# Where the low halves are made, and a fixed run of projections in front of the inverse's merging matmuls

## The chip, the core and the metric

The kernel runs on one NeuronCore of a Trainium2 chip. TensorE (PE in the profile) multiplies matrices, VectorE (DVE), ScalarE (ACT) and GpSimd (POOL) work element by element, and SyncE (SP) issues the DMA transfers. Time is device microseconds (us) of the whole program, the median of several runs.

## The reference, cut to what matters

The program is a hybrid block of two layers over 768 tokens (512 latent, 256 context) with 1024 channels. All four mixers read slices of one input projection:

```python
for layer in range(DEPTH):                 # DEPTH = 2
    need_ctx = layer < DEPTH - 1
    u_c, gate_c = modulate(h_ctx, cond_ctx, norm_w[layer], ada_w[layer], ada_b[layer])
    u_l, gate_l = modulate(h_lat, cond_lat, norm_w[layer], ada_w[layer], ada_b[layer])
    pc = split_in(u_c @ in_w[layer])
    pl = split_in(u_l @ in_w[layer])
    ya_c, ya_l = rwkv_branch(...)          # RWKV-7 on r, k, v
    ...                                    # SSD, Hyena, retention
    h_lat = h_lat + gate_l * merge_branches(u_l, ys_l, *mix_args)
```

The RWKV branch runs a recurrence over the tokens, and adds a bonus to what it reads out:

```python
def step(s, inp):
    r_t, w_t, kk_t, b_t, k_t, v_t = inp
    sa = -jnp.einsum('bhvk,bhk->bhv', s, kk_t)
    s = s * w_t[:, :, None, :] + sa[..., None] * b_t[:, :, None, :] + v_t[..., None] * k_t[:, :, None, :]
    return s, jnp.einsum('bhvk,bhk->bhv', s, r_t)
...
coef = jnp.sum(rwkv_heads(r)[:, :, None] * k_h * r_k, axis=(2, 4))
bonus = coef[..., None] * rwkv_heads(v)
```

## The kernel before, in words

**Projections.** `dense` multiplies the activations (kept as a high and a low half, `uh` and `ul`) by one 1024x128 block of weights at a time. `weights` loads half a block (256 KB, `wraw`), ScalarE casts it to the high half (`whi`, L185), and the engine `self.wl` subtracts it from the raw weights, which is the low half (`wlo`, L186). `self.wl` is GpSimd (`self.G`) while the projections are streamed, and VectorE in the merge at each layer's end. Three products (`whi` by `uh`, `whi` by `ul`, `wlo` by `uh`) are summed in PSUM: the 512 latent tokens in the tile `dl`, the 256 context tokens in `dc`. A projection of both segments is 24 matmuls of 128x512 and 24 of 128x256. `stream` then takes the result out of PSUM, with ScalarE alone (L436) or ScalarE and VectorE (L413, L425), and stores it.

**RWKV.** `rwkv_ct` handles one of four channel tiles (ct 0 to 3) per layer, in three stretches.
1. *Preparation:* VectorE and TensorE make the decayed keys and the blocks of A.
2. *Window:* VectorE turns A around (four transposes, L618), inverts all triangular 32x32 blocks by 60 dependent elimination operations (L622 and L623 in turn) and turns the result (L627 for `TT`, L632 for `TB`). The merging matmuls `cc<-TB,A` on TensorE can only start when `TB` is there.
3. *Chunk loop:* 12 chunks in series; each goes TensorE, ScalarE (`Rs`, L672), TensorE, ScalarE (L678), TensorE, VectorE (the state `Z`, L687 and L688), TensorE.

The bonus needs a head sum: a matmul with a matrix of ones (L370), one per segment, whose result VectorE multiplies by `v` (L609). The head sums lie in the PSUM tag `d1`, which has one buffer, so each one can be written only after the one before it was read. Layer 0 has two segments here, layer 1 only the first.

**What sets the order.** A scheduler of the framework orders the instructions of each engine; the order of the code is their priority, and `high_priority(offset=500)` pulls the splits ahead. Each engine then works through its list strictly in order. In the code, `rwkv` streams the next tile's k, r, v and the gate `ga` after each channel tile, and the 41 other projections of layer 0 after all four. Those carry the remaining modulation weights along (`each`): 64 loads of 256 KB (`adr`, four buffers), each cast by ScalarE (`adh`), subtracted by VectorE (`adl`) and used by two matmuls (L302, L303); two of them go with each projection.

Of the kernel before, what the change touches and what calls it, by code (L numbers as in the profile page):

```python
# [7 lines left out]
F32 = mybir.dt.float32  # L8
# [6 lines left out]
NOSYNC = mybir.DependencyInfo(mybir.DependencyClass.NoSync, mybir.DependencyReason.DATA)  # L15
# [124 lines left out]
class K:  # L140
# [56 lines left out]
            self.split(hi[:], lo[:], raw[:], leng=self.wl)  # L197
        return hi, lo

    def dense(self, srcs, uh, ul, segs, M=128):  # L200
        out = {t0: self.pst("dl" if n > 256 else "dc", [128, n]) for t0, n in segs}
        nk = len(srcs) * 4
        for j, src in enumerate(srcs):
            hi, lo = self.weights(src, 4, M)
            for t0, n in segs:
                for kk in range(4):
                    k = j * 4 + kk
                    for p, (w, u) in enumerate(((hi, uh), (hi, ul), (lo, uh))):
                        self.P.matmul(out[t0][:M, :n], w[:, kk, :], u[:, k, t0:t0 + n], start=(k == 0 and p == 0), stop=(k == nk - 1 and p == 2))  # L209
        return out  # L210

    def proj(self, l, ti, segs):
# [176 lines left out]
    def stream(self, l, need_ctx, items, each=None):  # L389

        V, S, G = self.V, self.S, self.G
        both = [(0, 512), (512, 256)]
        osegs = both if need_ctx else both[:1]

        def fg():
            return self.tile(self.fpool, [128, T], F32, "fg")

        for nm, j in items:
            sg = osegs if nm in ("r", "hy", "C", "rq", "ga", "gh", "zs", "gr", "mg") else both
            n1 = sg[-1][0] + sg[-1][1]  # L400
            if nm == "mg":
# [6 lines left out]
            ps = self.dense([src[:, 0:4], src[:, 4:8]], self.uh, self.ul, sg, M)  # L408
            g = fg()
            if nm in ("ga", "gh", "zs", "gr"):  # L410
                for t0, n in sg:
                    S.activation(out=g[:, t0:t0 + n], in_=ps[t0][:], func=AF.Tanh, scale=0.5)
                    V.scalar_tensor_tensor(out=g[:, t0:t0 + n], in0=g[:, t0:t0 + n], scalar=1.0, in1=ps[t0][:], op0=ALU.add, op1=ALU.mult)  # L413
            elif nm == "mg":
                self.gate(g, ps, sg, j)
            elif nm in ("r", "k", "v"):
                xp = self.padded(ps, sg)
                jj = "rkv".index(nm) * 4 + j
                t = fg()
                G.tensor_tensor(out=t[:, 0:512], in0=xp[:, 0:512], in1=xp[:, 2:514], op=ALU.add)  # L420
                if len(sg) > 1:
                    G.tensor_tensor(out=t[:, 512:768], in0=xp[:, 514:770], in1=xp[:, 516:772], op=ALU.add)
                for t0, n in sg:
                    S.activation(out=g[:, t0:t0 + n], in_=ps[t0][:], func=AF.Copy, scale=self.dc[:, jj:jj + 1])
                V.scalar_tensor_tensor(out=g[:, :n1], in0=t[:, :n1], scalar=self.dc[:, 12 + jj:13 + jj], in1=g[:, :n1], op0=ALU.mult, op1=ALU.add)  # L425
            elif nm == "hy":
                self.conv3(self.padded(ps, sg), sg, g, self.col("hcw", 3 * j), self.col("hcw", 3 * j + 1), self.col("hcw", 3 * j + 2), self.col("hcb", j))
            elif nm in ("x", "B", "C"):
                jj = dict(x=0, B=4, C=6)[nm] + j
                self.conv3(self.padded(ps, sg), sg, g, self.col("scw", 3 * jj), self.col("scw", 3 * jj + 1), self.col("scw", 3 * jj + 2), self.col("scb", jj))  # L430
                t = fg()
                S.activation(out=t[:, :n1], in_=g[:, :n1], func=AF.Tanh, scale=0.5)
# [5 lines left out]
            if each:  # L438
                each()
# [6 lines left out]
    def rwkv(self, l, need_ctx, pa, pb, items):  # L446
        segs = [(0, 512), (512, 256)]
        osegs = segs if need_ctx else segs[:1]
        self.load_rwkv(pb)
        for ct in range(4):  # L450
            y, no = self.rwkv_ct(l, ct, need_ctx, pa, pb, segs, osegs)
            self.stream(l, need_ctx, items[ct])
            self.apply_gate(self.fetch(l, "ga", ct, no, pb, "late"), y, no)
            self.nc.sync.dma_start(out=self.yd[0, ct, :, :no], in_=y[:, :no])

# [37 lines left out]

    def rwkv_ct(self, l, ct, need_ctx, pa, p, segs, osegs):
        V, S, G = self.V, self.S, self.G
        no = T if need_ctx else 512
        r = self.fetch(l, "r", ct, no, pa, "r")
        k = self.fetch(l, "k", ct, T, pa, "k")
# [768 lines left out]
    def run(self):  # L1267
        tc = self.tc

        def pool(name, side="left", **kw):  # L1270
            return tc.tile_pool(name=name, bufs=1, reuse_waits="tile", side=side, **kw)

        with tc.tile_pool(name="const", bufs=1) as self.cpool, tc.tile_pool(name="layer", bufs=1) as self.lpool, tc.tile_pool(name="w", bufs=1) as self.wpool, \
# [5 lines left out]
            self.pd = {n: [self.tile(dp, [c, 128, T] if n != "dt" else [16, T], F32, f"pd{n}{l}") for l in range(2)]  # L1279
                       for n, c in (("r", 4), ("k", 4), ("v", 4), ("ga", 4), ("hy", 12), ("x", 4), ("B", 2), ("C", 2), ("rq", 4), ("rk", 4), ("rv", 4),  # L1280
                                    ("gh", 4), ("zs", 4), ("gr", 4), ("dt", 1), ("mg", 32), ("lw", 8), ("la", 8))}
            self.load_consts()
            self.cols2 = [self.tile(self.lpool, [128, NCOLS], F32, f"cols{l}") for l in range(2)]
            self.modc = [self.tile(self.lpool, [128, 24, 2], F32, f"modc{l}") for l in range(2)]
# [4 lines left out]
            items = [[(n, c + 1) for n in "krv"] + [("ga", c)] for c in range(3)] + [[("ga", 3)]]  # L1289

            def some(**kw):
                return [(n, j) for n, c in kw.items() for j in range(c)]

            rest = some(rv=4, rk=4, rq=4, gr=4, gh=4, zs=4) + [("hy", 4 * j + c) for c in range(4) for j in range(3)] + some(dt=1, x=4, B=2, C=2)
# [10 lines left out]
            self.layer_cols(0)  # L1305
            for l in range(2):
                need = l == 0
                self.wl = self.G
                with pool(f"fill{l}") as self.fpool:
                    self.pb = self.PSUM_A  # L1310
                    with pool(f"psA{l}", space=PSUM) as self.psum:
# [24 lines left out]
                        with pool(f"ra{l}") as pa:  # L1336
                            with pool(f"rw{l}") as p:
                                self.rwkv(l, need, pa, p, items)
                        nmg = 0 if need else 2
                        if need:  # L1340
                            with pool("ada") as self.apool:
                                q, todo = [], list(adas)
# [5 lines left out]
                                        if q and (len(q) > 2 or not todo):  # L1348
                                            self.ada_step(*q.pop(0))

                                self.stream(l, need, rest[:4])
                                self.stream(l, need, rest[4:], each)
                                while q:
                                    each()
                        else:
                            self.stream(l, need, rest + [("mg", 24 + j) for j in range(nmg)])
# [54 lines left out]
```

## Time and profile before

| | |
|---|---|
| median of 3 runs | 3113.57 us (3111.22 to 3113.75) |
| the profiled execution | 3116.2 us, its span 3114.4 us |
| mean granted TensorE clock | 0.955 of full speed |
| TensorE busy | 2884.8 us (93%) |
| VectorE busy | 1861.3 us (60%) |
| ScalarE busy | 1174.5 us (38%) |
| GpSimd busy | 784.7 us (25%) |

The span is from the first to the last instruction on the core; 1.8 us of the device time lie around it. An engine counts as busy when it runs anything, at whichever clock. The granted clock (PEclk) is given as a share of full speed; the two levels are 1.2 and 2.4 GHz.

### The profile page before, as it was taken

How to read it: one execution, taken by the hardware profiler on the slowest of the kernel's cores; microseconds unless marked ns; L12 is line 12 of the kernel's file. 1: busy time of each engine (PE TensorE's matmuls, PEld its weight loads, DVE VectorE, ACT ScalarE, POOL GpSimd, SP SyncE). 2: the span in 40 equal slices, each digit the busy share in tenths (PEclk: the TensorE clock that was granted, in tenths of full speed). 3: DMA queues.
4: the chain of work that ended last, by engine and by line, in shares of the span. 5: the costliest groups of instructions: out<-in, count | busy, mean ns of one | idle time of the engine just before them, and what ended most of it. 6: DMA issues, size and time to landing. Idle time of an engine off the chain costs nothing. (4 is left out here: it accounts for less than half of the span.)

```text
span 3114.4 us, 48430 instructions
## 1 busy us (share of the span) xinstructions
PE 2884.8 (93%) x18708; PEld 2328.5 (75%) x18708; DVE 1861.3 (60%) x3288; ACT 1174.5 (38%) x2103; POOL 784.7 (25%) x906
## 2 busy tenths in 40 slices
PE   7998989898999999999999898798989899999898
PEld 3786767677767888777888867677767678877677
DVE  3358382846354577886725445837474535697875
ACT  4643332332354423334422454323333344243432
POOL 3523323232212200111012343332333332011111
PEclk9998989899999999999999988898989899999999
DMA  5542121211374333313425243312131234432434
GB/s 189 193 143 90 52 87 48 92 39 60 105 257 132 118 118 110 102 58 117 134 68 175 94 165 136 102 52 93 60 97 55 78 125 131 137 96 93 144 116 147
DMA packets 164266, 343.24 MB, mean 110 GB/s; under 512 B 19105, under 2 KB 28130, under 8 KB 164036
## 3 DMA queue, kind: packets, MB, share of 16 engines
q1 hardware_dynamic: 164036, 340.15, 33.2%
q8 instruction: 147, 2.41, 0.3%
q14 instruction: 83, 0.68, 0.1%
HBM read 254.77 MB, written 83.74 MB: 109 GB/s over the span
## 5 line engine op out<-in xcount | busy, mean ns | idle before, releaser
L209 PE MATMUL dl<-uh,whi 128*128 128x512 f32 (+1 forms) x1520 | 621.9, 409 | 11.3 <-DVE fg L413 7.1
L209 PE MATMUL dl<-ul,whi 128*128 128x512 f32 (+1 forms) x1520 | 623.9, 411 | 3.7 <-DVE ul L363 3.6
L209 PE MATMUL dl<-uh,wlo 128*128 128x512 f32 (+1 forms) x1520 | 620.3, 408 | 2.4 <-POOL wlo L186 2.4
L186 POOL TENSOR_TENSOR wlo<-wraw,whi 128x512 fp32r<-128x512 f32 (+1 forms) x256 | 348.6, 1363 | 787.7 <-ACT whi L185 693.4
L185 ACT CAST whi<-wraw 128x512 fp32r<-128x512 f32 x452 | 277.8, 615 | 613.4 <-PE dc L209 255.9
L209 PEld LDWEIGHTS dl<-uh,whi 128*128 128x128 f32 (+1 forms) x1520 | 290.8, 191 | 73.1 <-DVE fg L413 8.4
L209 PEld LDWEIGHTS dl<-ul,whi 128*128 128x128 f32 (+1 forms) x1520 | 290.7, 191 | 67.2 <-DVE ul L363 9.3
L209 PEld LDWEIGHTS dl<-uh,wlo 128*128 128x128 f32 (+1 forms) x1520 | 290.5, 191 | 65.9 <-POOL wlo L186 4.1
L209 PE MATMUL dc<-uh,whi 128*128 128x256 f32 (+1 forms) x960 | 282.7, 295 | 22.4 <-DVE fg L413 11.0
L209 PE MATMUL dc<-ul,whi 128*128 128x256 f32 (+1 forms) x960 | 279.4, 291 | 3.8 <-DVE ul L363 3.8
L209 PE MATMUL dc<-uh,wlo 128*128 128x256 f32 (+1 forms) x960 | 279.5, 291 | 0.0
L209 PEld LDWEIGHTS dc<-uh,whi 128*128 128x128 f32 (+1 forms) x960 | 185.3, 193 | 43.7 <-DVE fg L413 12.7
L1211 POOL TENSOR_TENSOR acc<-acc,fg 128x512 f32<-128x512 f32 x72 | 93.2, 1306 | 469.8 <-DVE fg L1210 469.3
L186 DVE TENSOR_TENSOR wlo<-wraw,whi 128x512 fp32r<-128x512 f32 x196 | 145.5, 743 | 107.9 <-ACT whi L185 106.2
L209 PEld LDWEIGHTS dc<-ul,whi 128*128 128x128 f32 (+1 forms) x960 | 185.2, 193 | 18.8 <-DVE ul L363 7.0
L687 DVE TENSOR_TENSOR Z<-cc,Z 128x256 f32<-128x256 f32 x80 | 33.9, 424 | 267.4 <-PE cc L174 267.1
L209 PEld LDWEIGHTS dc<-uh,wlo 128*128 128x128 f32 (+1 forms) x960 | 185.2, 193 | 5.1 <-issue 1.6
L817 POOL TENSOR_TENSOR m<-smask,adl 128x512 fp32r<-128x512 f32 x24 | 33.6, 1401 | 399.7 <-DVE adl L186 269.7
L672 ACT COPY Rs<-cc 64x256 f32<-64x256 f32 x96 | 35.3, 367 | 222.7 <-PE cc L174 221.7
L622 DVE TENSOR_TENSOR KB<-KB 128x30 f32<-128x30 f32 (+14 forms) x240 | 110.0, 458 | 6.4
L623 DVE TENSOR_TENSOR KB<-KB 128x30 f32<-128x30 f32 (+14 forms) x240 | 106.7, 445 | 6.6
L209 PE MATMUL dl<-yh,whi 128*128 128x512 f32 x256 | 103.5, 406 | 4.7 <-ACT yh L185 3.5
(412 smaller groups left out, 5927.9 us busy)
## 6 DMA issues: line engine op xcount, KB each, us to landing
wraw<-in_w SPq DMA_DIRECT2D x248, 256.0 KB, 2.7
wraw<-merge_w SPq DMA_DIRECT2D x128, 256.0 KB, 2.7
adr<-ada_w SPq DMA_DIRECT2D x96, 256.0 KB, 4.1
wraw<-branch_w SPq DMA_DIRECT2D x64, 256.0 KB, 2.7
wraw<-out_w SPq DMA_DIRECT2D x32, 256.0 KB, 3.9
pdlw<-fg SPq DMA_DIRECT2D x16, 384.0 KB, 2.3
pdla<-fg SPq DMA_DIRECT2D x16, 384.0 KB, 3.8
hfd<-Hs SPq DMA_DIRECT2D x16, 384.0 KB, 3.1
```

The costliest lines, as they stand in the source:

```text
L185: (heng or self.S).copy(out=hi, in_=src) if heng is None else heng.tensor_copy(out=hi, in_=src)
L186: (leng or self.V).tensor_tensor(out=lo, in0=src, in1=hi.bitcast(F32), op=ALU.subtract)
L209: self.P.matmul(out[t0][:M, :n], w[:, kk, :], u[:, k, t0:t0 + n], start=(k == 0 and p == 0), stop=(k == nk - 1 and p == 2))
L622: V.tensor_tensor(out=t3, in0=B[:, j + 1:32, j:j + 1].to_broadcast([128, ni, j]), in1=B[:, j:j + 1, 0:j].to_broadcast([128, ni, j]), op=AL ...
L623: V.tensor_tensor(out=B[:, j + 1:32, 0:j], in0=B[:, j + 1:32, 0:j], in1=t3, op=ALU.add)
L672: S.copy(out=Rs[hb], in_=Rp.t[hb])
L687: V.tensor_tensor(out=Zn[:], in0=Zp.t[:], in1=Z[:], op=ALU.add)
L817: eng.tensor_tensor(out=m2[:], in0=self.smask[:, d, :].unsqueeze(1).to_broadcast([128, 4, 128]), in1=ad[:, c, hs:hs + 4].bitcast(F32).unsq ...
L1211: G.tensor_tensor(out=acc[:, oc, t0:t0 + n], in0=acc[:, oc, t0:t0 + n], in1=g[:, t0:t0 + n], op=ALU.add)
```

## The change

It has four parts. The low halves of the streamed projections are made by VectorE. The projections come from one list (a generator, `feed`): k, r, v and `ga`, then six "light" ones per channel tile, then the rest. `fill(us)` issues projections worth that many us (by the formula in `dense_steps`) at a place of the code: one run of them before the bonus's head sum (80 or 54 in layer 0, 60 or 40 in layer 1), a second of 30 behind the transposes that end the inverse. From the head sum to the merging matmuls TensorE follows the order of the code (`manual_schedule`). `dc` becomes one bank used in alternating halves. And the modulation loads go only with those projections that are left when RWKV is done.

```diff
+    def dense_steps(self, out, srcs, uh, ul, segs, M=128):
+        for t0, n in segs:
+            if n > 256:
+                out[t0] = self.pst("dl", [128, n])
+            else:
+                self.ndc += 1
+                out[t0] = self.dcb[:, self.ndc % 2, :n]
...
+                        if n <= 256:
+                            if self.dcl is not None:
+                                self.tc.add_manual_dep(i.ins, self.dcl, NOSYNC, reason="bank order")
+                            self.dcl = i.ins.name
+                yield 12 * n / 2260
...
+    def fill(self, us):
+        while us > 0:
+            c = next(self.feed, None)
+            if c is None:
+                return
+            us -= c
+
+    def require(self, nm, j):
+        while (nm, j) not in self.parked:
+            next(self.feed)
...
             y, no = self.rwkv_ct(l, ct, need_ctx, pa, pb, segs, osegs)
-            self.stream(l, need_ctx, items[ct])
+            self.require("ga", ct)
...
+        self.fill((54 if ct else 80) if need_ctx else (40 if ct else 60))
+        region = self.tc.manual_schedule(engines={mybir.EngineType.PE})
+        region.__enter__()
         cb = self.headsum(ksum, osegs)
...
         V.transpose(out=TB[:].rearrange("p u s -> p s u"), in_=B.rearrange("p t s -> p s t"))
+        self.fill(30)
...
+        region.__exit__(None, None, None)
...
+            self.dcb = self.tile(self.psd, [128, 2, 256], F32, "dc")
...
-                self.wl = self.G
+                self.wl = self.V
...
+                        self.feed = self.stream_steps(l, need, items + [("mg", 24 + j) for j in range(nmg)])
+                        with pool(f"ra{l}") as pa, pool(f"rw{l}") as p:
+                            self.rwkv(l, need, pa, p)
...
-                                self.stream(l, need, rest[:4])
-                                self.stream(l, need, rest[4:], each)
+                                self.each = each
+                                for _ in self.feed:
+                                    pass
                                 while q:
                                     each()
```

TensorE, layer 0, ct 1: the head sum of the bonus (`d<-kd,bones`) for both segments. Before, the first segment stands in the chunk loop of the tile ahead, among its matmuls with `Z`:

```order
L209 MATMUL dl_4767<-uh_141,whi_950_4801 128x512
L209 MATMUL dl_4767<-ul_142,whi_950_4801 128x512
L370 MATMUL d_618_2858<-kd_576_2680,bones_113 128x512
L174 MATMUL cc_2020<-Z_2005,AR_1587 64x128
L174 MATMUL cc_2020<-Z_2005,AR_1680 64x128
```

The second segment stands 255 rows later, between the matmuls that make A, in the preparation.

```order
L174 MATMUL cc_2793<-AR_2777,KB_2778 128x128
L174 MATMUL cc_2804<-AR_2777,KB_2778 128x128 x2
L370 MATMUL d_619_2860<-kd_576_2680,bones_113 128x256
L174 MATMUL cc_2805<-AR_2777,KB_2778 128x128 x2
L174 MATMUL cc_2812<-AR_2777,KB_2778 128x128 x2
```

Now both stand in the window, one behind the other, with 63 projection matmuls of 128x512 and 72 of 128x256 ahead of them in the window and 96 and 84 behind them up to the merging matmuls.

```order
L215 MATMUL dc_111<-uh_142,whi_743_3916 128x256
L215 MATMUL dc_111<-ul_143,whi_743_3916 128x256
L215 MATMUL dc_111<-uh_142,wlo_744_3917 128x256
L386 MATMUL d_745_3946<-kd_650_3327,bones_114 128x512
L386 MATMUL d_746_3948<-kd_650_3327,bones_114 128x256
L215 MATMUL dl_3913<-uh_142,whi_752_4029 128x512
```

VectorE, the same tile: the bonus, which reads those head sums. Before, both readings stand ahead of the transposes that begin the window.

```order
L579 TENSOR_TENSOR A_2667<-cc_2805,maska_1543 128x256
L609 SCALAR_TENSOR_TENSOR bonus_2862<-d_619_2860,v_2649 128x256
L579 TENSOR_TENSOR A_2667<-cc_2812,maska_1543 128x512
L579 TENSOR_TENSOR A_2667<-cc_2813,maska_1543 128x512
L509 TENSOR_SCALAR et_3754<-d_761_3750 128x512
L618 STREAM_TRANSPOSE KB_2865<-A_2667 32x1024 x4
```

Now the first reading stands behind 51 of the 60 elimination operations (L661 and L662 are the old L622 and L623), and six low halves stand among them, the last one shown.

```order
L661 TENSOR_TENSOR KB_3953<-KB_3953 128x130
L186 TENSOR_TENSOR wlo_762_4101<-wraw_760_4098,whi_761_4100 128x512
L648 SCALAR_TENSOR_TENSOR bonus_3950<-d_745_3946,v_3296 128x512
L662 TENSOR_TENSOR KB_3953<-KB_3953 128x5x26
L661 TENSOR_TENSOR KB_3953<-KB_3953 128x108
L662 TENSOR_TENSOR KB_3953<-KB_3953 128x4x27
L648 SCALAR_TENSOR_TENSOR bonus_3950<-d_746_3948,v_3296 128x256
```

TensorE, layer 0, after RWKV: the modulation steps (`adh`, `adl` by `cs`). Before, four of their matmuls follow the 48 of each projection.

```order
L209 MATMUL dc_8326<-uh_141,wlo_1590_8360 128x256
L302 MATMUL d_1564_8226<-adh_8311,cs_54_133 4x512
L303 MATMUL d_1564_8226<-adl_8312,cs_54_133 4x512
L302 MATMUL d_1564_8226<-adh_8319,cs_54_133 4x512
L303 MATMUL d_1564_8226<-adl_8320,cs_54_133 4x512
L209 MATMUL dl_8413<-uh_141,whi_1601_8417 128x512
```

Now the last of them stand alone, pair behind pair, with little else between; the pattern goes on for some 36 of the 64 steps.

```order
L215 MATMUL dc_111<-uh_142,wlo_2422_11864 128x256
L319 MATMUL d_1591_9128<-adl_9142,cs_55_134 4x512
L318 MATMUL d_1591_9128<-adh_9149,cs_55_134 4x512
L319 MATMUL d_1591_9128<-adl_9150,cs_55_134 4x512
L318 MATMUL d_1591_9128<-adh_9157,cs_55_134 4x512
L319 MATMUL d_1591_9128<-adl_9158,cs_55_134 4x512
```

## Rows read from the trace of the kernel before

**Rows 1.** TensorE's waits: line, what it waited for, us in total, times, longest.

```profile
PE cc L174 <- DVE TB L632: 76.1, 8, 14.0
...
PE dc L209 <- DVE fg L413: 11.0, 4, 4.4
...
PE dc L209 <- ACT fg L436: 6.8, 4, 2.9
...
PE d L303 <- DVE adl L186: 3.8, 8, 0.8
```

**Rows 2.** Layer 0's windows: busy us (instructions) by engine; ct 0, ct 3, sum.

```profile
core 0: us, PE busy (x) PEld busy (x) DVE busy (x) ACT busy (x) POOL busy (x), PEclk, DMA share, GB/s
255.30:312.20 56.90, 42.25 (x212) 35.99 (x211) 52.67 (x87) 19.16 (x31) 19.93 (x19) 0.89 0.30 96
...
708.90:749.00 40.10, 29.42 (x169) 24.63 (x168) 38.14 (x74) 9.40 (x16) 9.19 (x9) 0.98 0.20 69
sum 194.00, PE 139.72 PEld 118.88 DVE 184.10 ACT 56.70 POOL 54.19; mean PE 34.93 PEld 29.72 DVE 46.02 ACT 14.18 POOL 13.55
```

**Rows 3.** Layer 0's chunk loops, the same view: ct 0, ct 3, sum.

```profile
312.20:388.80 76.60, 76.56 (x749) 61.09 (x750) 24.55 (x37) 22.91 (x52) 27.27 (x54) 0.92 0.15 51
...
749.00:822.20 73.20, 73.20 (x732) 57.57 (x733) 12.26 (x27) 19.68 (x47) 22.31 (x48) 0.92 0.12 41
sum 300.70, PE 300.61 PEld 237.83 DVE 79.36 ACT 85.21 POOL 102.38; mean PE 75.15 PEld 59.46 DVE 19.84 ACT 21.30 POOL 25.59
```

**Rows 4.** Layer 1's windows, the same view: ct 0 and sum.

```profile
1958.30:2014.50 56.20, 39.66 (x191) 32.06 (x190) 54.58 (x85) 20.76 (x36) 23.68 (x22) 0.87 0.30 97
...
sum 203.70, PE 147.67 PEld 118.94 DVE 196.54 ACT 66.29 POOL 71.76; mean PE 36.92 PEld 29.74 DVE 49.13 ACT 16.57 POOL 17.94
```

**Rows 5.** Layer 1's chunk loop of ct 0, the same view.

```profile
2014.50:2089.10 74.60, 74.53 (x696) 57.38 (x696) 20.22 (x34) 21.35 (x48) 27.95 (x53) 0.92 0.18 57
```

**Rows 6.** Timeline of the end of layer 0's window of ct 1: start, duration, instruction.

```profile
446.24 0.41 DVE L622 TENSOR_TENSOR KB<-KB 128x238 f32<-128x238 f32 x1
...
446.49 1.30 POOL L186 TENSOR_TENSOR wlo<-wraw,whi 128x512 fp32r<-128x512 f32 x1 [2.76 <-ACT whi L185]
...
446.68 1.38 DVE L623 TENSOR_TENSOR KB<-KB 128x238 f32<-128x238 f32 x1
...
447.03 0.39 PE L209 MATMUL dl<-uh,whi 128*128 128x512 f32 x1
...
447.26 0.40 PE L209 MATMUL dl<-ul,whi 128*128 128x512 f32 x1
...
448.09 0.40 DVE L622 TENSOR_TENSOR KB<-KB 128x234 f32<-128x234 f32 x1
...
454.82 0.29 DVE L623 TENSOR_TENSOR KB<-KB 128x130 f32<-128x130 f32 x1
...
457.28 1.90 DVE L627 STREAM_TRANSPOSE TT<-KB 128x1024 f32<-128x1024 f32 x1
...
461.14 2.77 PE L174 MATMUL cc<-TB,A 32*32 32x32 f32 x96 [13.49 <-DVE TB L632]
```

**Rows 7.** GpSimd's low halves (L186) in layer 0's four windows: sum.

```profile
sum 194.00, DVE 0.00 POOL 43.70; mean DVE 0.00 POOL 10.93
```

**Rows 8.** Groups by form: busy us, mean ns | idle before, releaser.

```profile
L186 DVE TENSOR_TENSOR wlo<-wraw,whi 128x512 fp32r<-128x512 f32 x196 | 145.5, 743 | 107.9 <-ACT whi L185 106.2 <-PE dc L209 0.2 <-PE dl L209 0.2
...
L618 DVE STREAM_TRANSPOSE KB<-A 32x1024 f32<-32x1024 f32 x32 | 64.5, 2015 | 3.7 <-PE cc L174 3.4
...
L687 DVE TENSOR_TENSOR Z<-cc,Z 128x256 f32<-128x256 f32 x80 | 33.9, 424 | 267.4 <-PE cc L174 267.1
```

**Rows 9.** The modulation loads: minimum, median, maximum ns; landing in us.

```profile
L185 ACT CAST adh<-adr x64: 605/619/626, 842.1 to 992.8; 128x512 fp32r<-128x512 f32 x64
L186 DVE TENSOR_TENSOR adl<-adr,adh x64: 669/685/1442, 842.7 to 994.5; 128x512 fp32r<-128x512 f32 x64
...
DMA to landing us min/median/max: 2.9/4.1/6.8
```

More of the change, by code (lines that the diff above doesn't have):

```diff
@@ L198, in weights @@
         return hi, lo
-    def dense(self, srcs, uh, ul, segs, M=128):
-        out = {t0: self.pst("dl" if n > 256 else "dc", [128, n]) for t0, n in segs}
+    def dense_steps(self, out, srcs, uh, ul, segs, M=128):
[5 more added lines that the diff above has]
+                out[t0] = self.dcb[:, self.ndc % 2, :n]
         nk = len(srcs) * 4
@@ L208, in dense @@
                     for p, (w, u) in enumerate(((hi, uh), (hi, ul), (lo, uh))):
-                        self.P.matmul(out[t0][:M, :n], w[:, kk, :], u[:, k, t0:t0 + n], start=(k == 0 and p == 0), stop=(k == nk - 1 and p == 2))
+                        i = self.P.matmul(out[t0][:M, :n], w[:, kk, :], u[:, k, t0:t0 + n], start=(k == 0 and p == 0), stop=(k == nk - 1 and p == 2))
+                        if n <= 256:
[3 more added lines that the diff above has]
+                yield 12 * n / 2260
+    def dense(self, srcs, uh, ul, segs, M=128):
+        out = {}
+        for _ in self.dense_steps(out, srcs, uh, ul, segs, M):
+            pass
         return out
@@ L387, in apply_gate, with stream, stream_steps @@
         self.V.scalar_tensor_tensor(out=y[:, :no], in0=g[:, :no], scalar=0.5, in1=y[:, :no], op0=ALU.mult, op1=ALU.mult)
-    def stream(self, l, need_ctx, items, each=None):
+    def fill(self, us):
[7 more added lines that the diff above has]
+            next(self.feed)
+    def stream(self, l, need_ctx, items):
+        for _ in self.stream_steps(l, need_ctx, items):
+            pass
+    def stream_steps(self, l, need_ctx, items):
         V, S, G = self.V, self.S, self.G
@@ L407, in stream @@
             M = 16 if nm == "dt" else 128
-            ps = self.dense([src[:, 0:4], src[:, 4:8]], self.uh, self.ul, sg, M)
+            ps = {}
+            yield from self.dense_steps(ps, [src[:, 0:4], src[:, 4:8]], self.uh, self.ul, sg, M)
             g = fg()
@@ L437, in stream @@
             self.nc.sync.dma_start(out=self.pd[nm][l][j, :, :n1] if nm != "dt" else self.pd[nm][l], in_=g[:M, :n1])
-            if each:
-                each()
+            self.parked.add((nm, j))
+            if self.each:
+                self.each()
     def fetch(self, l, nm, j, n, pool, tag):
@@ L444, in fetch, with rwkv @@
         return t
-    def rwkv(self, l, need_ctx, pa, pb, items):
+    def rwkv(self, l, need_ctx, pa, pb):
         segs = [(0, 512), (512, 256)]
@@ L495, in rwkv_ct @@
         V, S, G = self.V, self.S, self.G
+        for nm in "krv":
+            self.require(nm, ct)
         no = T if need_ctx else 512
@@ L1281, in run @@
                                     ("gh", 4), ("zs", 4), ("gr", 4), ("dt", 1), ("mg", 32), ("lw", 8), ("la", 8))}
+            self.dcb = self.tile(self.psd, [128, 2, 256], F32, "dc")
+            self.ndc, self.dcl = 0, None
             self.load_consts()
@@ L1288, in run @@
             self.cond()
-            items = [[(n, c + 1) for n in "krv"] + [("ga", c)] for c in range(3)] + [[("ga", 3)]]
             def some(**kw):
                 return [(n, j) for n, c in kw.items() for j in range(c)]
-            rest = some(rv=4, rk=4, rq=4, gr=4, gh=4, zs=4) + [("hy", 4 * j + c) for c in range(4) for j in range(3)] + some(dt=1, x=4, B=2, C=2)
+            light = some(rv=4, rk=4, rq=4, gr=4, gh=4, zs=4)
+            items = []
+            for c in range(4):
+                items += [(n, c + 1) for n in "krv" if c < 3] + [("ga", c)] + light[6 * c:6 * c + 6]
+            items += [("hy", 4 * j + c) for c in range(4) for j in range(3)] + some(dt=1, x=4, B=2, C=2)
             adas = [(l, j, k) for l, j0 in ((0, 4), (1, 0)) for j in range(j0, 6) for k in range(8)]
@@ L1307, in run @@
                 need = l == 0
-                self.wl = self.G
+                self.wl = self.V
+                self.parked, self.each = {(n, 0) for n in "krv"}, None
                 with pool(f"fill{l}") as self.fpool:
@@ L1335, in run @@
                                 list(self.hy_filters(1, need, p))
-                        with pool(f"ra{l}") as pa:
-                            with pool(f"rw{l}") as p:
-                                self.rwkv(l, need, pa, p, items)
                         nmg = 0 if need else 2
+                        self.feed = self.stream_steps(l, need, items + [("mg", 24 + j) for j in range(nmg)])
+                        with pool(f"ra{l}") as pa, pool(f"rw{l}") as p:
+                            self.rwkv(l, need, pa, p)
                         if need:
@@ L1349, in each @@
                                             self.ada_step(*q.pop(0))
-                                self.stream(l, need, rest[:4])
-                                self.stream(l, need, rest[4:], each)
+                                self.each = each
+                                for _ in self.feed:
+                                    pass
                                 while q:
                                     each()
+                                self.each = None
                         else:
-                            self.stream(l, need, rest + [("mg", 24 + j) for j in range(nmg)])
+                            for _ in self.feed:
+                                pass
                 acp = pool(f"acc{l}")
```

## Prediction

> **What bounds the kernel now.** I read the shares of the engines first: TensorE is busy for 93% of the span, so the time is TensorE's work plus two losses, its idle time and what the lower clock costs. Next I read its waits, to see which are large. By far the largest is that of the merging matmuls for `TB`: 76.1 us in 8 waits, one per channel tile, up to 14.0 [rows 1]. So I cut the span into windows (from the last preparing matmul to the merging matmuls) and chunk loops. In layer 0's four windows TensorE runs 139.7 of 194.0 us, so 54.3 are idle, while VectorE runs 184.1 [rows 2]; in layer 1 it is 147.7 of 203.7, 56.0 idle, VectorE 196.5 [rows 4]. There VectorE's chain sets the end. In the chunk loops TensorE is busy for 300.6 of 300.7 us [rows 3].
>
> The timeline of one window shows the cause: the last projection matmul starts at 447.26, VectorE goes on alone with the inverse, and merging begins at 461.14 [rows 6]. The projections given to this tile are used up too soon.
>
> The clock is the second loss. A stretch loses its length times what its PEclk lacks; PEclk mixes time at 2.4 GHz with time at 1.2 GHz. In layer 0 the window and the loop of ct 0 lose 56.9x0.11 + 76.6x0.08 = 12.4 us, those of ct 3 40.1x0.02 + 73.2x0.08 = 6.7 [rows 2, 3]; ct 0 of layer 1 loses 56.2x0.13 + 74.6x0.08 = 13.3 [rows 4, 5]. I take their mean, 10.8, for every tile, 43 in each layer, and 6.7 as the price of one cheap fall.
>
> **The windows of layer 0.** The matmuls of a projection start 0.23 us apart for 512 columns (447.03, 447.26 [rows 6]); half of that, 0.114, is my estimate for 256. By the order, TensorE has 178 and 168, 159 and 156, 159 and 156, 156 and 147 of them per window: 53 to 60 us each, while VectorE's work up to `TB` comes to 38 to 48 (below). So `TB` is ready before the merging matmuls, and that wait goes.
>
> But another takes its place. `d1` has one buffer, so the second segment's head sum waits until VectorE has read the first, and it stands in the fixed run, where nothing behind it can pass. VectorE's reading comes late. For ct 1, VectorE must do before it: four transposes, 4x2.015 = 8.1 [rows 8]; 51 of the 60 eliminations; six low halves, 6x0.743 = 4.5 [rows 8]; then the reading itself, 0.7. The eliminations: the last 26 take 457.28-448.09 = 9.2 us, the first 26 have the same sizes, and the 8 in the middle at 0.44 (446.24 to 446.68) make 3.5, in all 21.9; the nine left out take 457.28-454.82 = 2.5 [rows 6], so 19.4. Together 32.7, and VectorE begins 1.3 ahead of the window: 31.4. TensorE comes to the second head sum after 63x0.23 + 72x0.114 + 0.7 = 23.4. It stalls 8.0. In the same way ct 0 (all 60 eliminations, and 3.9 for `TT` and `TB`, ahead of the reading) gives 37.9-27.8 = 10.1; ct 2 (43 eliminations, five gate operations) 31.9-23.4 = 8.5; ct 3 (35, ten other operations) 30.2-21.7 = 8.5. That is 35. I add 5 for GpSimd's remaining interference and small waits: 40 idle against 54.3, a gain of 14.
>
> The clock falls in such stalls as it fell in the old gaps. Four falls at the price of ct 3 (dense work follows each) are 27 against 43, a gain of 16; the bounds are 0 (no better) and 43.
>
> **The windows of layer 1.** There is one segment, so no second head sum. TensorE's projections up to merging are 137 and 120 matmuls, 154 and 48, 154 and 0, 143 and 36: 45.2, 40.9, 35.4 and 37.0 us. VectorE is through `TB` after 8.1 + 21.9 + 3.9, the low halves (6, 9, 11, 11 at 0.743), 0.7 of bonus, and 0, 2, 5, 10 other operations at 0.5 to 1, less 1.3: 37.8, 41.9, 44.0, 46.5. The gaps are 0, 1.0, 8.6 and 9.5, with small waits 22 idle, against 56.0: a gain of 34. Two falls of the clock stay and two mostly go: 12 of the 43 gained, bounds 0 and 22.
>
> **The low halves on VectorE.** Each is cheaper there: GpSimd's last one took 1.30 us, VectorE's mean is 0.743 [rows 6, 8]. But they cost VectorE's time in a window that VectorE bounds; that is in the sums above. What they free is contention: the elimination operation at 446.68 took 1.38 us while GpSimd made a low half (446.49 to 447.79), and one of the same size took 0.41 just before [rows 6]. GpSimd's low halves were 43.7 of its 54.2 us in layer 0's windows [rows 2, 7].
>
> The Trainium skill (SBUF — State Buffer, "Who interferes with whom") states that a VectorE operation with two inputs in SBUF and a GpSimd operation that reads SBUF exclude one another, the later one waiting in full. The 1.38 beside 0.41 agrees. By that rule only the remaining 10.5 us of GpSimd could disturb the eliminations, the 5 I added would be about 2, and the result 3 us lower.
>
> Outside the windows VectorE now has them between the `Z` of the chunk loops: by the order 16, 15 and 14 between one window and the next in layer 0, 16, 18 and 16 in layer 1. VectorE waits 267.4/80 = 3.3 us ahead of each `Z` [rows 8], so most slip in. One that stands just ahead of `Z` delays the serial loop by up to 0.74, and the next tile's preparation, which leaves the windows, stands there too. I take 17 for both layers' loops and preparations; the bounds are 0 and 70 (these 95 at 0.743 in full).
>
> **The halves of `dc`.** In the built program each `dc` matmul still waits for the reading of the other half, so I put this at nothing. If the halves did work alone, the waits of `dc` for readings, 11.0 + 6.8 [rows 1], would go: 18 us more.
>
> **The modulation steps.** Before, each pair of them lay under a projection, and TensorE waited 3.8 us for their low halves [rows 1]. Now some 36 come with hardly a projection (7.5 us in all). Loads have four buffers, and a buffer is free when its subtraction is done: (4.1 + 0.62 + 0.69)/4 = 1.35 us a step [rows 9], while TensorE needs two matmuls, 0.46. So 36x1.35 = 49, less 36x0.46 + 7.5 = 24 of work, less the 4 of before: 21 lost. With the shortest landing (2.9) it is 10, with the longest (6.8) 45.
>
> **The sum.** Layer 0: 14 + 16; layer 1: 34 + 12; loops and preparations -17; modulation -21. That is 38 gained. The profiled execution took 3116.2 us and becomes 3078; it lies 2.6 above the median, so I forecast 3076.
>
> **The rivals.**
> - *VectorE becomes the bound (slower).* A low half on VectorE must wait for ScalarE's cast, and VectorE works strictly in order. In the merge it waited 107.9 us for 196 of them, 0.55 each [rows 8]. Some 125 of the moved ones stand in chunk loops and preparations. If each held up the serial loop in full, that is 69 more, 3145; half of it is 3110. It decides from 38 of the 69 on. For it: TensorE is never idle in the loops, so they have no spare time [rows 3]. Against it: the splits are pulled ahead, and VectorE idles 3.3 us before each `Z`. Chance 0.15.
> - *The fixed run covers everything.* If VectorE's reading of the first head sum is earlier than I add up, or the stall too short to lower the clock, layer 0's windows gain the other 40 and the 27 of the clock: 3076-67 = 3009. Against it: the order, in which 35 to 60 eliminations stand ahead of that reading. Chance 0.07.
> - *Layer 0 gains little and the modulation is dear.* If the stalls last nearly as long as the old gaps, with the clock's full price, the 30 of layer 0 shrink to 10, and if loads land in 5 us rather than 4.1, 36 steps cost 8 more: 3076+28 = 3104. For it: 64 loads now come in a burst, where before two went with each projection. Chance 0.18.
> - *The halves work after all.* 3076-18 = 3058. The Trainium skill (PSUM — Partial Sum Buffer, "PSUM bank collisions raise a hardware error") says that another address in the same bank collides as well, and that one guards by bank; by that rule the wait stays. No run shows it yet. Chance 0.05.
>
> **How the numbers follow.** The forecast has 0.55, with a range of its own from 3050 (loops free, clock better) to 3100 (modulation at its longest). The range for 8 in 10 leaves out the full cover at 3009 and the upper half of VectorE's rival: 3040 to 3125. Under 0.2% (6 us) a measurement can't tell from no change. All of the forecast's chance is faster, so are the cover and the halves, and half of the third rival: 0.55 + 0.07 + 0.05 + 0.09 = 0.76. Same: the other half of the third rival, near 3107, and the mildest part of the first: 0.10. Slower: 0.14.
>
> **What would show it.** Right: no wait for `TB` in layer 0; in each of its windows one wait of 8 to 10 us on VectorE's bonus at the head sum; gaps before merging in layer 1 only at ct 2 and ct 3, about 9 each; eliminations of 0.44 or less throughout; chunk loops 1 to 4 us longer; a stretch of some 45 us of modulation steps where TensorE waits for loads. Wrong: chunk loops longer by 6 us or more (the first rival), TensorE busy throughout the windows of layer 0 (the second), waits of `dc` for the gates gone (the fourth).

## The result

The changed kernel takes 3022.77 us (median of 4 runs, 3014.13 to 3026.65), the kernel before 3112.39 on the same occasions. The ratio is 0.9709, with a 95% interval of 0.9687 to 0.9731. The time fell by 90 us where 38 were forecast, and it lies below the range of 3040 to 3125.

The page's first two parts for the changed kernel show that TensorE's share rose, and that GpSimd lost 331 us of work while VectorE gained only 39. The clock row falls below 9 in two of its 40 slices; before (the last line) it did in nine.

```profile
span 3019.9 us, 48446 instructions
...
PE 2856.2 (95%) x18708; PEld 2299.8 (76%) x18708; DVE 1900.1 (63%) x3544; ACT 1187.5 (39%) x2109; POOL 453.3 (15%) x650
...
PEclk9999999999999899999999989999999999999999
...
PEclk9998989899999999999999988898989899999999
```

TensorE's waits in the changed kernel answer to [rows 1]: the wait for `TB` fell from 76.1 us in eight waits to 10.3 in two, and the forecast wait on the bonus is there, in four pieces.

```profile
PE d L386 <- DVE bonus L648: 22.6, 4, 8.1
...
PE cc L174 <- DVE TB L671: 10.3, 2, 6.3
```

The windows of the changed kernel, cut at the same places as [rows 2] and [rows 4] (layer 0's four, then layer 1's sum; columns as there), have 26.9 us of idle TensorE in layer 0 (before 54.3) and 18.4 in layer 1 (before 56.0).

```profile
245.40:316.90 71.50, 63.36 (x351) 54.76 (x349) 43.03 (x86) 20.25 (x37) 8.06 (x10) 0.95 0.28 93
416.20:482.60 66.40, 60.05 (x322) 50.89 (x320) 44.22 (x88) 20.98 (x37) 7.89 (x10) 0.95 0.28 91
581.80:644.90 63.10, 57.68 (x323) 48.39 (x321) 45.58 (x95) 15.82 (x28) 2.40 (x4) 1.00 0.29 95
746.20:810.40 64.20, 57.25 (x307) 48.57 (x306) 52.18 (x108) 24.50 (x42) 2.42 (x4) 0.95 0.26 87
sum 265.20, PE 238.34 PEld 202.61 DVE 185.01 ACT 81.55 POOL 20.77; mean PE 59.58 PEld 50.65 DVE 46.25 ACT 20.39 POOL 5.19
...
sum 184.90, PE 166.51 PEld 133.66 DVE 161.05 ACT 60.30 POOL 14.49; mean PE 41.63 PEld 33.41 DVE 40.26 ACT 15.07 POOL 3.62
```

Layer 0's chunk loops answer to [rows 3]. They last as long as before, at full clock now, and run 122 more instructions on TensorE, which are projections.

```profile
316.90:392.20 75.30, 75.30 (x774) 59.77 (x773) 35.10 (x54) 27.61 (x55) 19.06 (x46) 1.00 0.24 74
482.60:557.20 74.60, 74.60 (x766) 58.74 (x766) 36.54 (x57) 27.27 (x55) 20.62 (x46) 1.00 0.26 80
644.90:721.10 76.20, 76.19 (x776) 60.58 (x776) 39.91 (x60) 29.13 (x59) 21.90 (x45) 1.00 0.21 66
810.40:883.50 73.10, 73.10 (x761) 58.22 (x760) 19.64 (x40) 24.44 (x53) 15.39 (x41) 1.00 0.14 47
sum 299.20, PE 299.19 PEld 237.31 DVE 131.19 ACT 108.45 POOL 76.97; mean PE 74.80 PEld 59.33 DVE 32.80 ACT 27.11 POOL 19.24
```

Layer 1's loops did become longer, from 301.8 to 318.2 us in all (sum before, sum now). They run 129 more instructions on TensorE, 123 of them projections.

```profile
sum 301.80, PE 301.74 PEld 229.14 DVE 82.25 ACT 94.95 POOL 118.06; mean PE 75.43 PEld 57.28 DVE 20.56 ACT 23.74 POOL 29.51
...
sum 318.20, PE 316.03 PEld 241.22 DVE 151.39 ACT 126.37 POOL 87.00; mean PE 79.01 PEld 60.31 DVE 37.85 ACT 31.59 POOL 21.75
```

### The profile page after: what moved, and what is told of

Read it like the earlier page. It is cut to its first block, busy times and chain, and to the rows that moved or that the text cites. A ratio compares the mean times of both kernels' runs of the same rounds, so it can differ in the third digit from the quotient of the medians.

```text
span 3019.9 us, 48446 instructions
## 1 busy us (share of the span) xinstructions
PE 2856.2 (95%) x18708; PEld 2299.8 (76%) x18708; DVE 1900.1 (63%) x3544; ACT 1187.5 (39%) x2109; POOL 453.3 (15%) x650
## 5 line engine op out<-in xcount | busy, mean ns | idle before, releaser
L186 DVE TENSOR_TENSOR wlo<-wraw,whi 128x512 fp32r<-128x512 f32 x452 | 322.9, 715 | 302.1 <-ACT whi L185 269.4
L858 POOL TENSOR_TENSOR m<-smask,adl 128x512 fp32r<-128x512 f32 x24 | 33.6, 1402 | 583.1 <-DVE adl L186 459.0
L215 PE MATMUL dl<-yl,whi 128*128 128x512 f32 x256 | 104.4, 408 | 2.6 <-DVE yl L186 2.6
L215 PE MATMUL dl<-yh,wlo 128*128 128x512 f32 x256 | 104.4, 408 | 0.0
L701 POOL COPY UV<-vt 64x128 f32<-64x128 f32 x192 | 76.4, 420 | 182.3 <-ACT vt L634 176.6
```

What stands on the lines that cost most here:

```text
L186: (leng or self.V).tensor_tensor(out=lo, in0=src, in1=hi.bitcast(F32), op=ALU.subtract)
L215: i = self.P.matmul(out[t0][:M, :n], w[:, kk, :], u[:, k, t0:t0 + n], start=(k == 0 and p == 0), stop=(k == nk - 1 and p == 2))
L701: G.tensor_copy(out=UV[hk, d], in_=vt[d][hk, slot[d] // 2, :].rearrange("p (h x) -> p h x", h=2))
L858: eng.tensor_tensor(out=m2[:], in0=self.smask[:, d, :].unsqueeze(1).to_broadcast([128, 4, 128]), in1=ad[:, c, hs:hs + 4].bitcast(F32).unsq ...
```

## The experiments

Each ratio is against the kernel before, run beside it on the same chip. Where two runs are compared in us, the difference is that of their ratios times 3112; it is uncertain by 8 to 15 us.

### Which part brings the gain

**The low halves alone.** The kernel before with one line changed.

```diff
-                self.wl = self.G
+                self.wl = self.V
```

> The kernel before, with one edit: the streamed low halves on VectorE. Theory (two causes that add): GpSimd's low halves slowed the eliminations, and the runs of projections covered what was left. Then this half alone gives 30 to 40 us (eliminations at 0.44 us or less, lead and mixers some 15 together), so about 3075, and the wait for TB stays at 40 us or more. Rival A (nearly all of it is the removed contention): about 3030, wait for TB under 20. Rival B (nearly all of it is the runs of projections): within 10 of 3112.

Measured: 3022.07 us, ratio 0.9697 (0.9662 to 0.9733). This one line gives all that the whole change gives. TensorE's largest wait in this kernel is a third of what it was:

```profile
PE cc L174 <- DVE TB L632: 25.7, 8, 5.3
```

The costliest VectorE groups show the eliminations (240 operations a line; busy us, mean ns), before and in this kernel:

```profile
L622 DVE TENSOR_TENSOR KB<-KB 128x30 f32<-128x30 f32 (+14 forms) x240 | 110.0, 458 | 6.4
L623 DVE TENSOR_TENSOR KB<-KB 128x30 f32<-128x30 f32 (+14 forms) x240 | 106.7, 445 | 6.6
...
L623 DVE TENSOR_TENSOR KB<-KB 128x30 f32<-128x30 f32 (+14 forms) x240 | 81.6, 340 | 4.9
L622 DVE TENSOR_TENSOR KB<-KB 128x30 f32<-128x30 f32 (+14 forms) x240 | 80.9, 337 | 5.1
```

So 54 us left VectorE's chain in the eight windows, though eight and more low halves per window joined it. The sums of layer 0's windows, layer 1's windows, layer 0's loops and layer 1's loops, cut as before, show what that does to TensorE:

```profile
sum 182.70, PE 156.44 PEld 133.62 DVE 176.00 ACT 61.59 POOL 12.64; mean PE 39.11 PEld 33.41 DVE 44.00 ACT 15.40 POOL 3.16
...
sum 196.10, PE 162.45 PEld 133.55 DVE 189.01 ACT 74.50 POOL 11.27; mean PE 40.61 PEld 33.39 DVE 47.25 ACT 18.62 POOL 2.82
...
sum 302.20, PE 302.13 PEld 237.16 DVE 90.75 ACT 86.51 POOL 74.47; mean PE 75.53 PEld 59.29 DVE 22.69 ACT 21.63 POOL 18.62
...
sum 298.70, PE 298.68 PEld 223.56 DVE 97.47 ACT 93.61 POOL 76.91; mean PE 74.67 PEld 55.89 DVE 24.37 ACT 23.40 POOL 19.23
```

In the windows it is idle for 26.3 and 33.6 us, where it was for 54.3 and 56.0; the loops, in which VectorE now makes low halves too, are no longer than before (600.9 against 602.5). The time is rival A's, though its wait for `TB` (under 20) was put too low, and my theory's 3075 is wrong.

**The low halves back on GpSimd**, everything else as in the change.

```diff
-                self.wl = self.V
+                self.wl = self.G
```

> The changed kernel, with one edit: the streamed low halves back on GpSimd. By the theory of two causes it loses what the first gives alone, so about 3055 to 3065, with eliminations of 1 us and more while GpSimd works, and the wait at the head sum about as long as it was or longer. Rival A: about 3105. Rival B: within 10 of 3023.

Measured: 3055.32 us, ratio 0.9822 (0.9800 to 0.9844). Everything but the low halves therefore brings 55 us, the low halves alone 94, both together 90: they do not add. Here rival A fails, with its 3105, and the time is in the range of the two causes. So each cause works by itself, and they take the same waits: on top of the rest of the change, the low halves are worth 35. The eliminations are at a mean of 433 and 411 ns, and the wait at the head sum is 35.7 us against 22.6.

**One buffer for `dc` again**, in a bank of its own.

```diff
-                self.ndc += 1
-                out[t0] = self.dcb[:, self.ndc % 2, :n]
+                out[t0] = self.pst("dc", [128, n])
```

> The changed kernel, with dc as one buffer in a bank of its own, as before. Theory: the halves gain nothing, 3020 to 3026. Rival (the halves work after all, and account for a good part of the gain that was not forecast): 3035 to 3041, with waits of dc for the gates back at some 15 us.

Measured: 3019.45 us, ratio 0.9696 (0.9676 to 0.9716). The halves bring nothing that can be measured.

**No fixed order on TensorE**, the runs of projections kept.

```diff
-        region = self.tc.manual_schedule(engines={mybir.EngineType.PE})
-        region.__enter__()
...
-        region.__exit__(None, None, None)
```

> The changed kernel without the fixed order on TensorE: the runs of projections stay where the code issues them, but the scheduler orders head sum, projections and merging matmuls. By the order, the second head sum moves 7 to 14 rows back and the merging matmuls stay in their place. Theory (what counts is how many projections the code issues there, not that their order is fixed): 3014 to 3024, with waits at the head sum 1 to 2 us shorter per tile. Rival (the fixed order is needed to keep the projections in the window): 3040 or more.

Measured: 3008.27 us, ratio 0.9654 (0.9636 to 0.9672), faster than the change by 0.55%, some 17 us, and faster than I expected. The wait at the head sum is 15.5 us in three pieces, 7 less than in the change. The fixed order costs time; where the other 10 us come from is not shown.

### Contention, or only an earlier low half?

**GpSimd reads again.** To the first experiment's kernel I add one GpSimd subtraction per low half. Nobody reads its result, and it comes after the low half.

```diff
             self.split(hi[:], lo[:], raw[:], leng=self.wl)
+            if self.pb is self.PSUM_A:
+                jk = self.tile(self.wpool, [128, K, N], F32, "junk")
+                self.G.tensor_tensor(out=jk[:], in0=lo[:].bitcast(F32), in1=hi[:].bitcast(F32), op=ALU.subtract)
```

> The kernel of the first experiment (before, low halves on VectorE), and for each of its low halves GpSimd subtracts the same two halves once more into a tile that nobody reads. TensorE waits for nothing of it; only GpSimd's load on SBUF is back. Theory (contention between GpSimd's reads and VectorE's two-input operations is what the move removed): the eliminations' mean rises from some 0.36 us to 0.45 and more, the wait for TB from 26 us to 70 or more, and the time to 3095 to 3130. Rival (what counts is that the low half itself comes sooner, 0.7 instead of 1.4 us): 3015 to 3035.

Measured: 3130.41 us, ratio 1.0051 (1.0033 to 1.0069). The whole gain is gone. The eliminations are as slow as in the kernel before, or slower, and TensorE waits for `TB` again, though for less than the 70 us that I expected. It also waits longer for VectorE elsewhere: 18.4 us for low halves (7.7 in the first experiment) and 32.6 for VectorE's readings of `dl` and `dc` (16.1).

```profile
PE cc L174 <- DVE TB L635: 52.4, 8, 10.9
```

```profile
L626 DVE TENSOR_TENSOR KB<-KB 128x30 f32<-128x30 f32 (+14 forms) x240 | 114.1, 475 | 4.8
L625 DVE TENSOR_TENSOR KB<-KB 128x30 f32<-128x30 f32 (+14 forms) x240 | 110.6, 461 | 5.2
```

The timeline of a window of this kernel shows how it happens. The first operation of 150 columns takes 0.30 us; the second meets GpSimd's subtraction and takes 1.36, ending just after it; the next, of 168, takes 0.33.

```profile
434.63 0.30 DVE L625 TENSOR_TENSOR KB<-KB 128x150 f32<-128x150 f32 x1
434.85 1.30 POOL L200 TENSOR_TENSOR junk<-wlo,whi 128x512 f32<-128x512 f32 x1 [5.94 <-DVE wlo L186]
434.97 1.36 DVE L626 TENSOR_TENSOR KB<-KB 128x150 f32<-128x150 f32 x1
436.36 0.33 DVE L625 TENSOR_TENSOR KB<-KB 128x168 f32<-128x168 f32 x1
```

**GpSimd writes instead**, again in the first experiment's kernel.

```diff
+            if self.pb is self.PSUM_A:
+                jk = self.tile(self.wpool, [128, 448], F32, "junk")
+                a, b = lo[:, 0, 0:1].bitcast(F32), hi[:, 0, 0:1].bitcast(F32)
+                self.G.tensor_tensor(out=jk[:, 0:1], in0=a, in1=b, op=ALU.subtract)
+                self.G.memset(jk[:], 0.0)
+                self.G.memset(jk[:], 0.0)
+                self.G.memset(jk[:], 0.0)
+                self.G.tensor_tensor(out=jk[:, 0:1], in0=a, in1=b, op=ALU.subtract)
```

> As the run in which GpSimd read the two halves again, but now GpSimd only writes for as long: for each low half two subtractions of one column (one ahead, one behind, so that GpSimd holds the halves for as long as there) and three fills of a tile of 448 columns between them, some 1.5 us in all. Theory (it is GpSimd's reads that hold VectorE up): eliminations at a mean of 0.36 us or less, 3018 to 3035. Rival 1 (any work of GpSimd holds VectorE up): means of 0.45, 3100 to 3130. Rival 2 (holding the halves keeps TensorE's weights waiting): eliminations quick, but 3060 or more.

Measured: 3029.51 us, ratio 0.9727 (0.9697 to 0.9758). The eliminations and the first of GpSimd's three fills in this kernel:

```profile
L631 DVE TENSOR_TENSOR KB<-KB 128x30 f32<-128x30 f32 (+14 forms) x240 | 81.4, 339 | 4.8
L630 DVE TENSOR_TENSOR KB<-KB 128x30 f32<-128x30 f32 (+14 forms) x240 | 79.7, 332 | 5.2
```

```profile
L202 POOL MEMSET junk<- 128x448 f32 x256 | 122.7, 479 | 15.2 <-POOL junk L201 0.2
```

GpSimd is busy for longer than in the run before it (978.8 us against 816.7), holds the halves at least as long, and VectorE's eliminations are as quick as without it. It is the reads that block. The Trainium skill (SBUF — State Buffer, "Who interferes with whom") says this: a VectorE operation with two inputs in SBUF excludes a GpSimd operation that reads SBUF, and not one that only writes. These two runs agree, at 3130 and 3030 us.

### What the rest of the change cost

**ScalarE reads the head sum.**

```diff
-            V.scalar_tensor_tensor(out=bonus[:, t0:t0 + n], in0=cb[t0][:, :n], scalar=0.5, in1=v[:, t0:t0 + n], op0=ALU.mult, op1=ALU.mult)
+            S.activation(out=bonus[:, t0:t0 + n], in_=cb[t0][:, :n], func=AF.Copy, scale=0.5)
+        V.tensor_tensor(out=bonus[:, :no], in0=bonus[:, :no], in1=v[:, :no], op=ALU.mult)
```

> The changed kernel, with one edit: ScalarE takes the bonus's head sums out of PSUM, and VectorE multiplies later from SBUF. Theory: the 22.6 us at the second head sum go with the clock's fall behind them (some 8), and nothing takes their place, since TB is ready long before TensorE is through its projections: about 2993. Rival (the stall only moves on, to the merging matmuls or to a wait for weights): 3010 to 3023, with a new wait of some 20 us in layer 0's windows.

Measured: 3021.88 us, ratio 0.9711 (0.9693 to 0.9729): no gain, as the rival had it. In layer 0 TensorE now waits for ScalarE, 21.1 us in six waits, where it waited 22.6 for VectorE:

```profile
PE d L386 <- ACT bonus L648: 10.6, 4, 7.5
...
PE dc L215 <- ACT xp L273: 5.4, 1, 5.4
PE dc L215 <- ACT fg L457: 5.1, 1, 5.1
```

The timeline of ct 0's window shows the 7.5. ScalarE's reading stands behind the copy of `TT`, which waits for VectorE's inverse, and that is the same chain. In ct 1 and ct 3 the head sum is read early, but ScalarE's next readings of projections stand behind that copy (it begins at 448.26 and at 783.51), which makes the other two waits.

```profile
275.70 1.04 ACT L669 COPY TT<-TT 32x1024 f32<-32x1024 f32 x1 [5.98 <-DVE TT L667]
276.76 0.60 ACT L648 ACTIVATE bonus<-d 128x512 f32<-128x512 f32 x1
```

**Head sum ahead of the first run**, outside the fixed order.

```diff
-        self.fill((54 if ct else 80) if need_ctx else (40 if ct else 60))
-        region = self.tc.manual_schedule(engines={mybir.EngineType.PE})
-        region.__enter__()
         cb = self.headsum(ksum, osegs)
         ...
+        self.fill((54 if ct else 80) if need_ctx else (40 if ct else 60))
+        region = self.tc.manual_schedule(engines={mybir.EngineType.PE})
+        region.__enter__()
```

> The changed kernel, with the head sum and the bonus ahead of the first run of projections, and out of TensorE's fixed order. Theory (the stall at the head sum is real time, and in the run in which ScalarE read it, it only became a wait for ScalarE): the wait at the head sum is under 3 us, layer 0's windows are idle for 5 us together, and the time is 2993 to 3003. Rival (projections are a fixed stock: what the windows save, a later stretch lacks): 3012 to 3024.

Measured: 3004.95 us, ratio 0.9647 (0.9626 to 0.9669), between the two expectations: 0.62% or 19 us better than the change, near the 22.6 of the wait. The wait at the head sum is gone from the list of waits; those for ScalarE's readings of `dc` grew from 6.5 to 17.6 us (L469 and L457).

**Five modulation loads per projection.**

```diff
-                                    for _ in range(2):
+                                    for _ in range(5):
```

> The changed kernel, with five modulation loads per projection instead of two, so that hardly any are left when the projections end. Theory (the bare tail of 33 steps costs 10 to 15 us): 3008 to 3013. Rival (the loads then hold up the projections' own weights on the DMA queue): 3020 to 3035, with TensorE waiting for ScalarE's casts between 900 and 1000 us.

Measured: 2999.74 us, ratio 0.9631 (0.9610 to 0.9651): 0.78% or some 24 us better than the change, give or take 9. That is what the bare tail cost, where the expectation had 10 to 15 and the prediction 21. In the profile TensorE is idle for 13.3 us less than in the change and busy for 8.8 less.

**Both, and a shorter second run in layer 0.**

```diff
-        self.fill(30)
+        self.fill(14 if need_ctx else 30)
```

> The two edits above together, and in layer 0 the second run of projections cut from 30 us to 14, so that the rest stays for later. Theory (the windows of layer 0 hold more projections than VectorE's chain needs, once the head sum does not stop them): the gains add, 2980 to 2992, and merging waits for TB under 3 us per tile in layer 0. Rival (the cut run leaves a gap ahead of merging again): 3000 to 3012, waits for TB of 5 us and more.

Measured: 2973.55 us, ratio 0.9545 (0.9527 to 0.9563): 51 us better than the change, the best of all, and below the expected 2980. The two edits gave 19 and 24 by themselves, so 8 are left for the shorter run, which was not tried alone and which these times can't tell from nothing. Layer 0's windows in this kernel (columns as in [rows 2]) are idle for 13.4 us, and shorter than in either kernel:

```profile
240.90:292.60 51.70, 46.35 (x255) 40.23 (x253) 37.88 (x79) 14.77 (x26) 4.31 (x6) 0.97 0.29 96
395.50:431.40 35.90, 35.90 (x205) 31.11 (x205) 33.84 (x73) 8.95 (x15) 1.50 (x3) 1.00 0.26 85
...
sum 175.00, PE 161.62 PEld 138.79 DVE 151.38 ACT 48.09 POOL 10.77; mean PE 40.41 PEld 34.70 DVE 37.85 ACT 12.02 POOL 2.69
```

**The best one with its low halves on GpSimd.**

```diff
-                self.wl = self.V
+                self.wl = self.G
```

> The best kernel so far (head sum first, five modulation loads, second run of 14), with the low halves back on GpSimd. If contention and the runs of projections fill the same waits, then even without the stall at the head sum and the tail of modulation steps the move to VectorE is worth less here than the 92 that it gave alone: 3015 to 3040 against 2974. If the parts add, it is 3060 or more.

Measured: 3022.39 us, ratio 0.9711 (0.9690 to 0.9731). So the move is worth 52 us here and 94 alone. Contention and a lack of projections feed the same waits, and whichever is mended first takes most of what is there.

**The best one with longer first runs in layer 1.**

```diff
-        self.fill((54 if ct else 80) if need_ctx else (40 if ct else 60))
+        self.fill((54 if ct else 80) if need_ctx else (48 if ct else 64))
```

> The best kernel so far, with longer first runs in layer 1 (64 and 48 us instead of 60 and 40). If merging there still waits for TB because TensorE has too few projections (10.2 us in two waits), these waits shrink by 6 or more and the time is 2962 to 2970. Rival (the projections are taken from the chunk loops and the rest, which run short instead): 2971 to 2980.

Measured: 2977.05 us, ratio 0.9559 (0.9537 to 0.9580), no different. The wait for `TB` left the list of the largest, and the time did not follow: the rival's case, as far as the times tell.

## Why the prediction was wrong

The direction and most mechanisms held; the sum was less than half of the result. By its own terms (clock by the prediction's formula, length times what PEclk lacks):

| term | forecast, us | measured, us |
|---|---|---|
| layer 0's windows, idle | 14 | 54.3 - 26.9 = 27.4 |
| layer 0's clock | 16 | 43 - 10 = 33 |
| layer 1's windows, idle | 34 | 56.0 - 18.4 = 37.6 |
| layer 1's clock | 12 | 43 - 15 = 28 |
| loops and preparations | -17 | about 0 (by the first experiment: 739.1 before, 738.1) |
| modulation steps | -21 | -24 (by the run with five loads) |
| lead before the first window | 0 | 255.3 - 245.4 = 9.9 |

The measured terms together come to 112, more than the 90. The clock formula also counts slow time in which TensorE idles, which costs nothing. TensorE's totals close the sum without it: for the same 18708 matmuls it is idle for 65.9 us less (229.6 before, 163.7 now) and busy for 28.6 less (2884.8 and 2856.2). The windows make up 65.0 of the first. The second is about what all changes of the clock came to, with the slow tail of modulation steps (0.74 from 1000 to 1040) counted against them; how it divides was not resolved.

**The bound.** Right: VectorE's chain set the end of each window. But the prediction read the chain as work that must be covered with more projections. A quarter of the eliminations' time was not work: 216.7 us in the kernel before, 162.5 once GpSimd stopped reading.

**"The low halves on VectorE"** is the step that failed. It saw the contention (1.38 us beside 0.41), and the windows' sums used undisturbed eliminations: 21.9 us for a window's 60, which measured 27.1 before (216.7 over eight windows) and 20.3 without GpSimd's reads. But the price of the move by itself was never worked out. The gain of the windows was put down to the projections, "used up too soon", and what the move got as a term of its own was a loss of 17 in loops and preparations, and outside the sum a gain of 3 for less interference. The runs showed the reverse. The move alone gives 94 us and nearly halves the idle time of the windows; the rest alone gives 55, and next to nothing on top of the move. The 17 was no loss: with the low halves on VectorE, and little else changed, loops and preparations take 738.1 us, before 739.1, with 26 more projection matmuls in the loops and a granted clock there some 0.01 higher. The lead was put at nothing and gained 9.9, of which 7.5 come with the move alone (its end at 247.8). The excess was there to be read: the 240 operations of a line had a mean of some 450 ns beside a median of some 355, and after the move 340 beside 348.

**The stall at the head sum.** The mechanism was right, the size too large: 22.6 us in four waits (8.1, 6.4, 2.3 and 5.8 for ct 0 to 3), where 35 were forecast (10.1, 8.0, 8.5 and 8.5). In ct 1 VectorE came sooner than added up. In its window, from 416.2, the reading starts at 445.62, 29.4 in, while the sum had 30.7 (31.4 less the reading's 0.7). The rows of that place, TensorE and VectorE, with the matmuls behind the stall 0.42 us apart instead of 0.23:

```profile
438.98 1.02 PE L386 MATMUL d<-kd,bones 128*128 128x512 f32 x2
...
445.62 0.68 DVE L648 SCALAR_TENSOR_TENSOR bonus<-d,v 128x512 f32<-128x512 f32 x1
...
446.35 1.22 PE L386 MATMUL d<-kd,bones 128*128 128x256 f32 x2 [6.35 <-DVE bonus L648]
...
448.23 0.63 PE L215 MATMUL dl<-uh,wlo 128*128 128x512 f32 x1
...
448.65 0.63 PE L215 MATMUL dl<-uh,whi 128*128 128x512 f32 x1
```

**The clock.** In size this term missed most: 28 were forecast for both layers, and the same formula gives 61. Of the four falls that I left in layer 0, three are in the trace (0.95 in three windows, 1.00 in that of ct 2, whose stall was 2.3 us), and each ends inside the window, among projections. The loops of layer 0 are at 1.00 throughout, where they were at 0.89 to 0.93. Priced at 6.7 each they were to cost 27; by the rows it is (71.5 + 66.4 + 64.2)x0.05 = 10.

**Layer 1's windows.** The size was right, 37.6 against 34, and `TB` is waited for at ct 2 and ct 3 only. These gaps are half of the forecast (4.0 and 6.3 where 8.6 and 9.5 were added up), and ct 0 has one of 6.3 us that was not forecast, on ScalarE's reading of `dc`.

**The modulation steps and the halves of `dc`.** Both right: some 24 us against 21, with 33 bare steps in 43 us (989 to 1032), 1.30 each against 1.35; and nothing. What the prediction cites for the halves from the Trainium skill (PSUM — Partial Sum Buffer, "PSUM bank collisions raise a hardware error") is borne out as far as the time goes.

**The rivals.** The sign of the first, loops longer by 6 us or more, did come in layer 1 (82.1 us from 73.6 at ct 1, 82.8 from 76.5 at ct 2). But the low halves alone left layer 1's loops at 298.7 us, and TensorE is busy for 316.0 of the 318.2 us that they take now, which points to the projections that moved in and not to VectorE as their bound. That the fixed run covers everything did not come, though the time is near that case by luck: the stall was there, and the time came from elsewhere.

## What to carry to other kernels

When VectorE bounds a stretch, compare the mean of its short two-input operations with their median; if they differ, look for a GpSimd operation that reads SBUF beside the long ones, and move that work before planning how to cover the wait. Measure each part of a change alone: here one line gave it all, and the rest, which covers the same waits, paid on top of it only after the head sum and the tail of modulation steps had been mended and a run shortened (3022.8 to 2973.6 us). A wait moved to another engine is not gone if that engine's list has, ahead of it, work that waits for the same chain.

## What the runs showed of the hardware

A GpSimd subtraction of 128x512, whose result is not used, cost some 0.44 us of the whole program each (ratio 1.0051 against 0.9697, 110 us over 252 of them). GpSimd work that only writes, and lasts longer, cost 9 us in all (0.9727 against 0.9697), which these runs can't tell from nothing.

The hold-up goes both ways. In the run in which GpSimd reads again, half of its subtractions take 1.30 us or less, like the one shown above, which held an elimination up. But the one at 426.90, which began during a VectorE operation of 128x768 (426.82, 0.95 us), took 2.02, and the elimination behind it 1.32. The longest took 4.33 (316.38), beside three VectorE operations of 128x768 in a row.
